# Decay sums by a scan, wider score products, and w_out buffers in turn, in a one-layer hybrid decoder step

## The chip, the cores and the metric

The kernel runs on one core of a Trainium2 chip. The metric is the device time of one execution in microseconds (us), the median of several runs. TensorE multiplies matrices (PE in the profile, with its weight loads as PEld), VectorE (DVE) and ScalarE (ACT) work elementwise, GpSimd (POOL) copies and fills, and SyncE (SP) issues most DMA transfers. PE writes to PSUM; the other engines move results from there to SBUF.

## The reference

One layer of a decoder on 512 prompt tokens and 8 × 4 sample tokens, in fp32: a half-step SwiGLU FFN, a mixing stage, and a second FFN, each closed by a layer norm. The mixing stage projects each token to `r`, `k`, `v`, low-rank gates and a short convolution's inputs, and runs a recurrence over time in each of 8 heads of 64 features:

```python
w_log = -softplus(-(w0 + tanh(wd) @ w_lora_up)) - 0.5
decay = exp(-exp(w_log))                  # = exp(-exp(-0.5) * sigmoid(w0 + tanh(wd) @ w_lora_up))
a = sigmoid(a0 + ad @ a_lora_up)
kk = k * k_k;  kk = kk / max(norm(kk), 1e-12)
S = S * decay + (S @ -kk) (kk * a)^T + v k^T       # per token and head
o = S @ r
```

The heads' outputs are normalised, gated, joined with the convolution's and multiplied by `w_out`.

## The kernel before

Features lie on the 128 partitions and the 544 token columns on the free axis; time columns are handled in halves of 256 and 288. To keep fp32 accuracy, each large operand is split in a high and a low part (`hl` for weights: ACT copies the high part, DVE subtracts for the low part, lines 146 and 147), and three products are summed. Weights come raw by DMA into `raw` tiles, and their split goes to the next `hl` tile of a ring: three base tiles, and extra ones while other memory is free. The ring's counter is `wstate["hl"]`.

PSUM has two rings: `mm` with three buffers (function `big`) and `sm` with five (function `sm`). A buffer is taken again only when its contents have been moved out.

The middle stage (about 395 to 728 us of the span) does the recurrence in chunks of 64 tokens, eight chunks and one set of sample columns. Its heads are taken in four pairs; the two heads of a pair (two "parities") lie in the lower and upper 64 partitions. For each pair the class `Pair` has these steps:

- `gates`: the decay's logits and `a`, from the low-rank rows `T12` and the weights `lo`. The decay's logits have time on the partitions; `w0`, copied to all partitions by a DMA, is added by DVE. ACT takes sigmoids (`sw`, `sws` for samples, `a`).
- `square`: the key's norm. ACT squares `k`, PE sums over a head, DVE takes a maximum; the tile is `kq`.
- `decays`: sums of the sigmoids within a chunk, as products of `sw` with triangular matrices `tri` and `tris`, then exponentials of both signs (`Pi`, `Pn`).
- `prep`: nine DVE instructions that scale key and `r` by them: `at`, `O`, `AR` for the samples, and `bkb`.
- `scores`: for each chunk and parity, `bkb` (weights) times `at` and times `O`. DVE masks the result from PSUM into `SC`, then scales `bkb` in place; PE then transposes `v` and the scaled `bkb`, and ACT moves those out (`UV`, `BK`).

Projections `project` run between these steps: `own_a(p+1)` (gates, k, square, r of the next pair) before `scores(p)`, `own_b(p+1)` (decays, prep, v) behind it. Pieces of projections or convolution are taken as fill between the pinned score steps. The program gives PE's order for pinned parts; for the rest the framework's scheduler sets each engine's order. Within an engine instructions run in the order set.

Behind the last scores come a triangular inverse on DVE with the sample tokens and the convolution beside it (`elim`, `sample`), the chain of eight chunks (`chain`), and `w_out` with the norm of the heads (`wout`, `gnorm`). Eight `w_out` weight blocks (`wc`, `wr`) are loaded and split there.

Of the kernel before, what the change touches and what calls it, by code (L numbers as in the profile page):

```python
# [61 lines left out]
def body(ctx: ExitStack, tc: tile.TileContext, xT, gu1, wd1, win, wo_c, wo_r, gu2, wd2, lora, w0, vec, cst,  # L62
# [764 lines left out]
    class Pair:  # L827
# [4 lines left out]
        def gates(self):  # L832
            p, fc = self.p, self.fc
            self.sw = sw = p2.tile([P, 4, P], F32, name="sw")
            self.sws = sws = p2.tile([64, P], F32, name="sws")
# [1 line left out]
            q, q2, qa = sm(), sm(), []
            for (t0, t1, h) in SEG:
                qa.append(sm())
                PE.matmul(qa[h][:, :t1 - t0], lo[64:128, 0, fc], T12[64:128, t0:t1], start=True, stop=True)  # L840
# [3 lines left out]
            DVE.tensor_tensor(sw, q.rearrange("p (t f) -> p t f", t=4), w0b[:, None, fc].to_broadcast([P, 4, P]), op=OP.add)  # L844
            DVE.tensor_tensor(sws, q2[0:64, 0:P], w0b[0:64, fc], op=OP.add)
            for t0, t1, h in SEG:
                ACT.activation(a[:, t0:t1], qa[h][:, :t1 - t0], AF.Sigmoid, bias=col(V_A0, p))
            ACT.activation(sw, sw, AF.Sigmoid)
            self.sg = ACT.activation(sws, sws, AF.Sigmoid)
# [9 lines left out]
        def decays(self):  # L859
            p, kq = self.p, self.kq  # L860
            Pi = p2.tile([P, 600], F32, name="Pi")
            self.Pn = Pn = p2.tile([P, 576], F32, name="Pn")
# [9 lines left out]
            ln_exp(self.sg, lambda: ACT.activation(pi[:, :, 1:65], s64(q), AF.Exp, scale=-CDEC))
            ACT.activation(ps_[:, :, 1:5], s4(q2[:, 0:64]), AF.Exp, scale=-CDEC)
            ACT.activation(Pn[:, 0:512], q, AF.Exp, scale=CDEC)
            ACT.activation(Pn[:, 512:576], q2[:, 0:64], AF.Exp, scale=CDEC)
# [1 line left out]
            ACT.activation(kq, kq, AF.Exp, scale=-0.5)
# [4 lines left out]
        def prep(self):
            p, nk, a, Pn = self.p, self.kq, self.a, self.Pn
            pi, ps_ = self.pi, self.ps
            self.at = at = p2.tile([P, 512], F32, name="at")
# [8 lines left out]
            DVE.tensor_tensor(O[:, p, 0:8, :], s64(rf[:, :512]), pi[:, :, 1:65], op=OP.mult)
# [5 lines left out]
            DVE.scalar_tensor_tensor(Pn, rf, col(V_RK, p), kf, op0=OP.mult, op1=OP.mult)  # L900
# [466 lines left out]
def _constants():  # L1367
# [77 lines left out]
```

## Time and profile before

| | us |
|---|---|
| median of three runs | 1105.9 (1105.31 to 1106.1) |
| the profiled execution | 1107.86 |
| its span | 1106.1 |
| PE busy | 1078.5 |
| DVE busy | 833.0 |
| ACT busy | 570.7 |
| gates of pair 0 to its scores | 406.5 to 432.3 |
| scores of pairs 1, 2, 3 begin | 468.0, 504.4, 528.6 |
| inverse, samples, convolution end | 601.2 |
| chunk chain ends | 645.5 |

In rows of the timeline a line has start, length, engine, source line, operation, output and inputs, shapes, count, and in square brackets the idle time before it with what ended it. A PE matmul in fp32 appears as two records. The names `T` and `cpb` in the gates' rows are the tiles `T12` and `lo`.

### The profile page before, as it was taken

How to read it: one execution, taken by the hardware profiler on the slowest of the kernel's cores; microseconds unless marked ns; L12 is line 12 of the kernel's file. 1: busy time of each engine (PE TensorE's matmuls, PEld its weight loads, DVE VectorE, ACT ScalarE, POOL GpSimd, SP SyncE). 2: the span in 40 equal slices, each digit the busy share in tenths (PEclk: the TensorE clock that was granted, in tenths of full speed). 3: DMA queues.
4: the chain of work that ended last, by engine and by line, in shares of the span. 5: the costliest groups of instructions: out<-in, count | busy, mean ns of one | idle time of the engine just before them, and what ended most of it. 6: DMA issues, size and time to landing. Idle time of an engine off the chain costs nothing.

```text
span 1106.1 us, 22515 instructions
## 1 busy us (share of the span) xinstructions
PE 1078.5 (98%) x9176; PEld 1035.7 (94%) x9176; DVE 833.0 (75%) x1520; ACT 570.7 (52%) x1042; POOL 201.9 (18%) x320
## 2 busy tenths in 40 slices
PE   9999999999999999999999999999999999999996
PEld 8999999999999998999879789899999999999995
DVE  7788888888875757668576477768889788886655
ACT  6645555564553575644222564467555556554524
POOL 0121221312100022212141610001312223031000
PEclk9999999999999999999999999999999999999998
DMA  8567594957742232122525333133957759495402
GB/s 289 123 134 193 120 221 102 213 143 163 187 126 91 95 107 68 39 68 70 135 70 152 126 111 115 49 105 77 212 140 160 177 125 214 126 196 132 115 1 81
DMA packets 81977, 142.98 MB, mean 129 GB/s; under 512 B 20432, under 2 KB 44368, under 8 KB 81616
## 3 DMA queue, kind: packets, MB, share of 16 engines
q1 hardware_dynamic: 54672, 105.35, 29.9%
q0 software_dynamic: 27200, 36.18, 21.0%
q8 instruction: 72, 1.18, 0.4%
q14 instruction: 33, 0.27, 0.1%
HBM read 123.65 MB, written 8.95 MB: 120 GB/s over the span
## 4 chain that ended last, share of the span: by engine, by line
PE 78%; DMA 7%; DVE 6%; ACT 4%; issue 4%; SPq 0%; POOL 0%; ACTq 0%; DVEq 0%; POOLq 0%
PE mm L75 50%; PE sm L75 29%; DMA z<-cpb 2%; DMA raw<-in_gu 2%; DVE hl L147 2%; ACT hl L146 2%; DMA z<-sv 1%; DMA raw<-in_wo_r 1%; DVE hhl L151 1%; DMA raw<-in_wd 1%; DMA z<-in_xT 1%; DVE z L609 0%; SPq L697 0%; DMA BK<-in_w 0%; ACT z L252 0%
## 5 line engine op out<-in xcount | busy, mean ns | idle before, releaser
L75 PE MATMUL mm<-xhl,hl 128*128 128x288 f32 (+2 forms) x2640 | 367.9, 294 | 0.9 <-ACT xhl L150 0.5
L75 PEld LDWEIGHTS mm<-xhl,hl 128*128 128x128 f32 x2640 | 344.7, 190 | 13.2 <-issue 5.4
L147 DVE TENSOR_TENSOR hl<-raw,hl 128x1024 fp32r<-128x1024 f32 (+3 forms) x224 | 261.0, 1170 | 67.7 <-ACT hl L146 66.7
L146 ACT ACTIVATE hl<-raw 128x1024 fp32r<-128x1024 f32 (+3 forms) x224 | 224.6, 1012 | 92.0 <-DVE raw L486 31.3
L75 PE MATMUL sm<-xhl,hl 128*128 128x272 f32 (+1 forms) x1392 | 193.8, 289 | 1.0 <-ACT xhl L150 0.7
L75 PEld LDWEIGHTS sm<-xhl,hl 128*128 128x128 f32 x1392 | 182.3, 189 | 2.2 <-ACT xhl L150 1.4
L75 PE MATMUL mm<-tv,hl 128*128 128x272 f32 x864 | 121.5, 289 | 4.1 <-ACT cpb L580 2.1
L75 PE MATMUL mm<-hhl,hl 128*128 128x272 f32 (+2 forms) x792 | 119.2, 294 | 0.1
L75 PEld LDWEIGHTS mm<-tv,hl 128*128 128x128 f32 x864 | 113.6, 189 | 5.2 <-ACT cpb L580 3.0
L75 PEld LDWEIGHTS mm<-hhl,hl 128*128 128x128 f32 x792 | 105.9, 188 | 5.1 <-ACT sv L625 1.5
L75 PE MATMUL sm<-hhl,hl 128*128 128x272 f32 (+2 forms) x792 | 109.6, 288 | 0.0
L75 PEld LDWEIGHTS sm<-hhl,hl 128*128 128x128 f32 x792 | 103.0, 188 | 0.5
L492 POOL DMA_DIRECT2D raw<-in_gu x36 | 43.5, 1209 | 258.4 <-DVE cpb L582 83.4
L498 POOL DMA_DIRECT2D raw<-in_wd x32 | 39.3, 1467 | 274.5 <-DVE hlb L151 240.2
L75 PE MATMUL mm<-tv,hlb 128*128 128x272 f32 x432 | 61.1, 291 | 0.7 <-ACT cpb L589 0.7
L75 PEld LDWEIGHTS mm<-tv,hlb 128*128 128x128 f32 x432 | 56.4, 188 | 2.3 <-ACT cpb L589 2.2
L150 ACT ACTIVATE hhl<-sv 128x272 fp32r<-128x272 f32 (+1 forms) x52 | 26.0, 513 | 30.3 <-DVE sv L349 12.1
L151 DVE TENSOR_TENSOR hlb<-raw,hlb 128x512 fp32r<-128x512 f32 x52 | 35.8, 688 | 5.6 <-ACT hlb L150 5.5
L150 ACT ACTIVATE hhl<-hk 128x272 fp32r<-128x272 f32 (+1 forms) x48 | 24.2, 505 | 27.5 <-DVE hk L556 12.9
L217 ACT ACTIVATE lnq<-z 128x512 f32<-128x512 f32 (+1 forms) x24 | 15.1, 654 | 42.9 <-DVE z L216 42.9
L486 DVE TENSOR_TENSOR raw<-raw 128x512 f32<-128x512 f32 x52 | 35.8, 689 | 1.0
L75 PE MATMUL mm<-hhl,hlb 128*128 128x272 f32 (+2 forms) x264 | 36.4, 288 | 0.0
(300 smaller groups left out, 1373.0 us busy)
## 6 DMA issues: line engine op xcount, KB each, us to landing
raw<-in_gu SPq DMA_DIRECT2D x84, 512.0 KB, 4.8
raw<-in_gu POOLq DMA_DIRECT2D x36, 512.0 KB, 6.4
raw<-in_wd SPq DMA_DIRECT2D x32, 512.0 KB, 4.6
raw<-in_win SPq DMA_DIRECT2D x26, 512.0 KB, 3.6
raw<-in_wd POOLq DMA_DIRECT2D x32, 256.0 KB, 6.4
raw<-in_wd SPq DMA_DIRECT2D x16, 384.0 KB, 3.2
z<-cpb POOLq DMA_DIRECT2D x16, 272.0 KB, 9.1
z<-sv POOLq DMA_DIRECT2D x16, 272.0 KB, 6.6
```

The costliest lines, as they stand in the source:

```text
L75: ins = f(*args, **kw)
L146: ACT.activation(hl[:, 0, a:b], raw[:, a:b], AF.Copy)
L147: DVE.tensor_tensor(hl[:, 1, a:b], raw[:, a:b], hl[:, 0, a:b].bitcast(F32), op=OP.subtract)
L150: ACT.activation(hi, x, AF.Copy)
L151: DVE.tensor_tensor(lo, x, hi.bitcast(F32), op=OP.subtract)
L217: sq = ACT.activation(qq, zz, AF.Square)
L486: DVE.tensor_tensor(y[:, :, 0], y[:, :, 1], a[:, :, 1], op=OP.add)
L492: POOL.dma_start(x.rearrange("p (s c) -> p s c", s=2), bass.AP(tensor=a11.tensor, offset=a11.offset, ap=[[2 * D, P], [P * 2 * D, 2], [1, 5 ...
L498: POOL.dma_start(four(x)[:, i], bass.AP(tensor=a11.tensor, offset=a11.offset, ap=[[DFF, P], [P * DFF, 2], [1, 256]]), accum_op=OP.add)
```

## The change

1. **Gates and decays.** The decay's logits are made in feature rows, as `a` already was, by two products of 256 and 320 columns. `w0` comes as a bias per feature of the sigmoid, so its DMA and the two additions on DVE go. One `tensor_tensor_scan` on DVE over 128x576 then sums the sigmoids along time: it multiplies the running sum by `cm`, which is 0 at each chunk's start and 1 elsewhere, and adds the next element. The triangular products and the constants for them go; `Exp` reads SBUF, and `Pn` is one instruction in place of two.
2. **Scores.** `at` and `O` lie in one tile `AO` (row 0 and rows 1 to 4), and each chunk and parity has one product with 128 columns, made of two strided pieces of 64, in place of two with 64.
3. **Value transposes** take one `mm` and one `sm` buffer in place of two `sm`.
4. **`own_a`** puts the first half of the `r` projection ahead of `square`.
5. **`wstate["hl"]`** is set to 0 ahead of the w_out loads and again ahead of the second FFN, so these blocks begin with the base tiles.

```diff
     def gates(self):
-            self.sw = sw = p2.tile([P, 4, P], F32, name="sw")
-            self.sws = sws = p2.tile([64, P], F32, name="sws")
+            self.sg = sg = p2.tile([P, 576], F32, name="sg")
...
-                for t in (2 * h, 2 * h + 1):
-                    PE.matmul(q[:, t * P:(t + 1) * P], T12[0:64, t * P:(t + 1) * P], lo[0:64, 0, fc], start=True, stop=True)
-            PE.matmul(q2[0:64, 0:P], T12[0:64, 512:576], lo[0:64, 0, fc], start=True, stop=True)
-            DVE.tensor_tensor(sw, q.rearrange("p (t f) -> p t f", t=4), w0b[:, None, fc].to_broadcast([P, 4, P]), op=OP.add)
-            DVE.tensor_tensor(sws, q2[0:64, 0:P], w0b[0:64, fc], op=OP.add)
...
+            for t0, t1, _ in SEG:
+                qw, qa = sm(), sm()
+                PE.matmul(qw[:, :t1 - t0], lo[0:64, 0, fc], T12[0:64, t0:t1], start=True, stop=True)
+                PE.matmul(qa[:, :t1 - t0], lo[64:128, 0, fc], T12[64:128, t0:t1], start=True, stop=True)
+                ACT.activation(sg[:, t0:t1], qw[:, :t1 - t0], AF.Sigmoid, bias=col(V_W0, p))
+                self.last = ACT.activation(a[:, t0:t1], qa[:, :t1 - t0], AF.Sigmoid, bias=col(V_A0, p))
+            DVE.tensor_tensor_scan(sg, cm, sg, 0.0, op0=OP.mult, op1=OP.add)
     def decays(self):
-            q = sm()
-            for t in range(4):
-                PE.matmul(q[:, t * P:(t + 1) * P], self.sw[:, t, :], tri, start=True, stop=True)
-            q2 = sm()
-            PE.matmul(q2[:, 0:64], self.sws, tris, start=True, stop=True)
...
+            ln_exp(self.last, lambda: ACT.activation(pi[:, :, 1:65], s64(self.sg[:, 0:512]), AF.Exp, scale=-CDEC))
+            ACT.activation(ps_[:, :, 1:5], s4(self.sg[:, 512:576]), AF.Exp, scale=-CDEC)
+            ACT.activation(Pn, self.sg, AF.Exp, scale=CDEC)
     def scores(self):
-                    for i, x in enumerate((at, O[:, p])):
-                        for par, q in enumerate(qs):
-                            PE.matmul(q[:, c * P + 64 * i:c * P + 64 * i + 64], bkb[R(par), a0c + c, :, :],
-                                      x[R(par), a0c + c, :], start=True, stop=True)
+                    for par, q in enumerate(qs):
+                        PE.matmul(q[:, c * P:c * P + P], bkb[R(par), a0c + c, :, :], AO[R(par), 0:p + 2:p + 1, a0c + c, :],
+                                  start=True, stop=True)
...
             for a0c, n in ((0, 5), (5, 4)):
-                qs = (sm(), sm())
+                qs = (big(), sm())
     def own_a(p):
+        yield from project(i + 1, p, 0, rf)
         yield from act(pairs[p].square)
-        yield from seq(*(project(i + 1, p, h, rf) for h in range(2)))
+        yield from project(i + 1, p, 1, rf)
...
+    wstate["hl"] = 0
     wc = [wload(wo_c[i]) for i in range(4)]
     wr = [wload(wo_r[i]) for i in range(4)]
...
     drain()
+    wstate["hl"] = 0
     wstate["ex_hl"] = []
```

The edits also move instructions. The first place is PE from the gates of pair 0 to those of pair 1. Before:

```order
L75 MATMUL sm<-T_4312,cpb 128x256
L75 MATMUL sm<-cpb,T_4312 128x128 x2
L75 MATMUL sm<-T_4312,cpb 128x320
L75 MATMUL sm<-cpb,T_4312 128x128 x2
L75 MATMUL sm<-cpb,T_4312 64x128
L75 MATMUL sm<-kq,cs 128x256
L75 MATMUL sm<-kq,cs 128x320
L75 MATMUL mm<-xhl,hl 128x288 x7
L75 MATMUL sm<-cs,sw 128x128 x4
L75 MATMUL sm<-cs,sws 128x64
L75 MATMUL mm<-xhl,hl 128x288 x17
L75 MATMUL sm<-T_4312,cpb 128x256
```

and with the change:

```order
L76 MATMUL sm<-T_4312,cpb 128x256 x2
L76 MATMUL sm<-T_4312,cpb 128x320 x2
L76 MATMUL sm<-kq,cs 128x256
L76 MATMUL sm<-kq,cs 128x320
L76 MATMUL mm<-xhl,hl 128x288 x24
L76 MATMUL sm<-T_4312,cpb 128x256 x2
```

The triangular products between the 7 and the 17 projection products are gone, and the time-row products (`cpb,T`) are feature-row products of the form that `a` had.

The second place is DVE at the scores of pair 1 (`SC` rows), with steps of pair 2 around them; `kq` and `r` are pair 2's. Before:

```order
L857 TENSOR_SCALAR kq<-sm 128x320
L786 SCALAR_TENSOR_TENSOR r<-pb,vc,dt 128x256
L887 SCALAR_TENSOR_TENSOR kq<-k,vc,kq 128x576
L786 SCALAR_TENSOR_TENSOR r<-pb,vc,dt 128x256
L790 SCALAR_TENSOR_TENSOR r<-pb,vc,dt 128x32
L147 TENSOR_TENSOR hl<-raw,hl 128x1024
L917 TENSOR_TENSOR SC<-sm,cs 128x512 x2
L147 TENSOR_TENSOR hl<-raw,hl 128x1024
L917 TENSOR_TENSOR SC<-sm,cs 128x512 x2
L917 TENSOR_TENSOR SC<-sm,cs 128x128 x2
L921 TENSOR_TENSOR bkb<-bkb,Pe 128x1024
```

and the same place with the change:

```order
L854 TENSOR_SCALAR kq<-sm 128x320
L877 SCALAR_TENSOR_TENSOR kq<-k,vc,kq 128x576
L879 SCALAR_TENSOR_TENSOR AR_4711<-kq,Pi 128x64
L787 SCALAR_TENSOR_TENSOR r<-pb,vc,dt 128x256
L791 SCALAR_TENSOR_TENSOR r<-pb,vc,dt 128x32
L884 TENSOR_TENSOR AO<-r,Pi 128x512
L885 TENSOR_TENSOR AR_4711<-r,Pi 128x64
L148 TENSOR_TENSOR hl<-raw,hl 128x1024
L905 TENSOR_TENSOR SC<-sm,cs 128x512 x4
L905 TENSOR_TENSOR SC<-sm,cs 128x128 x2
L909 TENSOR_TENSOR bkb<-bkb,Pe 128x1024
```

`AO<-r,Pi` (the former `O<-r,Pi`) and two small `AR` steps of pair 2 stand ahead of the score evictions; before, they stood behind `bkb<-bkb,Pe`. The weight split that stood between the evictions is gone from there, and one stands ahead of them as before. At the scores of pair 0 a split stands between the evictions in both kernels, at those of pair 2 none does with the change.

More of the change, by code (lines that the diff above doesn't have):

```diff
@@ L50 @@
 V_MU, V_A0, V_KK, V_KA, V_RK, V_GNG, V_GNB, V_CW = 48, 62, 66, 70, 74, 78, 82, 86
-NV = 98
-C_ONES, C_ID, C_MASK, C_MASKS, C_TRI, C_TRIS, C_BO, C_CEN, C_BM, C_OFF = 0, 128, 192, 320, 448, 576, 640, 768, 896, 904
-NCST = 968
+V_W0 = 98
+NV = 102
+C_ONES, C_ID, C_MASK, C_MASKS, C_BO, C_CEN, C_BM = 0, 128, 192, 320, 448, 576, 704
+NCST = 712
 def R(par):
@@ L61, in body @@
 @with_exitstack
-def body(ctx: ExitStack, tc: tile.TileContext, xT, gu1, wd1, win, wo_c, wo_r, gu2, wd2, lora, w0, vec, cst,
+def body(ctx: ExitStack, tc: tile.TileContext, xT, gu1, wd1, win, wo_c, wo_r, gu2, wd2, lora, vec, cst,
          sst, cstate, s0, y_o, wkvp_o, wkvs_o, shift_o, conv_o):
@@ L810, in body @@
     bo, cen, ident, msk, msks = (csl(c, n) for c, n in ((C_BO, P), (C_CEN, P), (C_ID, 64), (C_MASK, 128), (C_MASKS, 128)))
-    tri, tris, bmask, _ = csl(C_TRI, 128), csl(C_TRIS, 64, slice(0, 64)), csl(C_BM, 8), csl(C_OFF, 64)
-    O = tl([P, 4, NC_, 64], F32, name="O")
+    bmask = csl(C_BM, 8)
+    AO = tl([P, 5, NC_, 64], F32, name="AO")
+    at, O = AO[:, 0, 0:8], AO[:, 1:5]
     AR8 = tl([P, 4, 2, 64], F32, name="AR8")
@@ L820, in body @@
     UV = rc([P, 4, 2, NC_, 64], F32, name="UV")
-    w0b = BK[:, 3].rearrange("p a c t -> p (a c t)")[:, 0:512]
-    dma(w0b, bass.AP(tensor=w0.tensor, offset=w0.offset, ap=[[0, P], [1, 512]]))
+    cm = p2.tile([P, 576], F32, name="cm")
+    POOL.memset(cm, 1.0)
+    POOL.memset(cm[:, 0:512:64], 0.0)
+    POOL.memset(cm[:, 512:576:4], 0.0)
     Ad = dr.tile([2, 32, 65, 64], F32, name="Ad")
@@ L833, in gates @@
             p, fc = self.p, self.fc
-            self.sw = sw = p2.tile([P, 4, P], F32, name="sw")
-            self.sws = sws = p2.tile([64, P], F32, name="sws")
+            self.sg = sg = p2.tile([P, 576], F32, name="sg")
             self.a = a = p2.tile([P, 576], F32, name="a")
[L837 to L840, printed above, removed]
-                for t in (2 * h, 2 * h + 1):
-                    PE.matmul(q[:, t * P:(t + 1) * P], T12[0:64, t * P:(t + 1) * P], lo[0:64, 0, fc], start=True, stop=True)
-            PE.matmul(q2[0:64, 0:P], T12[0:64, 512:576], lo[0:64, 0, fc], start=True, stop=True)
[L844 to L849, printed above, removed]
+            for t0, t1, _ in SEG:
[5 more added lines that the diff above has]
+            DVE.tensor_tensor_scan(sg, cm, sg, 0.0, op0=OP.mult, op1=OP.add)
         def square(self):
@@ L871, in decays @@
             POOL.memset(ps_[:, :, 0], 1.0)
[L872 to L875, printed above, removed]
+            ln_exp(self.last, lambda: ACT.activation(pi[:, :, 1:65], s64(self.sg[:, 0:512]), AF.Exp, scale=-CDEC))
+            ACT.activation(ps_[:, :, 1:5], s4(self.sg[:, 512:576]), AF.Exp, scale=-CDEC)
+            ACT.activation(Pn, self.sg, AF.Exp, scale=CDEC)
             ACT.activation(kq, kq, AF.Ln)
@@ L884, in prep @@
             pi, ps_ = self.pi, self.ps
-            self.at = at = p2.tile([P, 512], F32, name="at")
             self.bkb = bkb = p2.tile([P, NC_, 2, 64], F32, name="bkb")
             DVE.scalar_tensor_tensor(nk, kf, col(V_KK, p), nk, op0=OP.mult, op1=OP.mult)
-            DVE.scalar_tensor_tensor(s64(at), s64(nk[:, :512]), -1.0, pi[:, :, 0:64], op0=OP.mult, op1=OP.mult)
+            DVE.scalar_tensor_tensor(at, s64(nk[:, :512]), -1.0, pi[:, :, 0:64], op0=OP.mult, op1=OP.mult)
             DVE.scalar_tensor_tensor(s4(AR8[:, p, 0, :]), s4(nk[:, 512:]), -1.0, ps_[:, :, 0:4], op0=OP.mult, op1=OP.mult)
             for par in range(2):
-                POOL.tensor_copy(UV[R(par), p, par, 0:8, :], s64(at)[R(par)])
+                POOL.tensor_copy(UV[R(par), p, par, 0:8, :], at[R(par)])
             DVE.tensor_tensor(nk, nk, a, op=OP.mult)
@@ L903, in scores @@
             p, bkb, vf = self.p, self.bkb, vfs[self.p]
-            at = s64(self.at)
             for a0c, n in ((0, 4), (4, 4), (8, 1)):
@@ L1376, in _constants @@
     blk = np.kron(np.eye(2), np.ones((64, 64)))
-    c[:, C_TRI:C_TRI + 128] = blk * np.tile(incl, (2, 2))
-    c[0:64, C_TRIS:C_TRIS + 64] = incl & same
     c[:, C_CEN:C_CEN + 128] = np.eye(P) - blk / 64
```

4 lines of the change are left out of this document (1 added, 3 removed).

## The prediction

> **What bounds the kernel now.** I read the page's busy shares first, then the chain of waits as shares by engine.
>
> ```profile
> PE 1078.5 (98%) x9176; PEld 1035.7 (94%) x9176; DVE 833.0 (75%) x1520; ACT 570.7 (52%) x1042; POOL 201.9 (18%) x320
> PE 78%; DMA 7%; DVE 6%; ACT 4%; issue 4%; SPq 0%; POOL 0%; ACTq 0%; DVEq 0%; POOLq 0%
> ```
>
> TensorE is nearly always busy, but an average over 1106 us says little about the stages that the change touches. So next the busy times by stretch: the run-up to the scores of head pair 0, one row from each pair's scores to the next pair's, the chunk chain, and the first half of w_out. The columns are length, then busy time and count of PE, weight loads, DVE, ACT and POOL, then clock, DMA share, GB/s.
>
> ```profile
> 406.50:432.30 25.80, 23.34 (x175) 21.22 (x174) 16.75 (x31) 17.08 (x35) 7.67 (x21) 1.00 0.17 52
> 432.30:468.00 35.70, 35.46 (x326) 33.09 (x325) 22.79 (x39) 19.72 (x44) 7.97 (x26) 1.00 0.18 53
> 468.00:504.40 36.40, 36.16 (x332) 33.79 (x331) 23.61 (x40) 19.54 (x42) 6.56 (x25) 1.00 0.22 67
> 504.40:528.60 24.20, 23.99 (x241) 22.58 (x241) 21.83 (x38) 10.85 (x24) 6.67 (x14) 1.00 0.26 61
> 601.20:645.50 44.30, 41.27 (x936) 35.96 (x935) 20.57 (x60) 21.96 (x67) 23.81 (x58) 1.00 0.28 88
> 645.50:682.50 37.00, 35.84 (x249) 32.85 (x247) 31.05 (x65) 22.83 (x43) 0.00 (x0) 1.00 0.37 118
> ```
>
> From 432 to 528 PE leaves under 0.3 us idle per row: what is taken from PE there comes off the end, unless a new wait eats it. In the first row PE idles 2.46 us, and the chain of waits names why:
>
> ```profile
> 406.62 3.28 DMA BK<-in_w
> 428.93 0.78 ACT kq L853
> ```
>
> The w0 rows arrive 3.3 us after PE needs them, everything of pair 0 on DVE and ACT is late by that, and PE ends up waiting at 429.75 for the square of pair 1's key. PE's own timeline around pair 0:
>
> ```profile
> 406.52 0.48 PE L75 MATMUL sm<-T,cpb 64*128 64x256 f32 x1
> 407.33 0.43 PE L75 MATMUL sm<-T,cpb 64*128 64x320 f32 x1
> 408.05 1.24 PE L75 MATMUL sm<-kq,cs 128*128 128x256 f32 x4
> 411.40 1.16 PE L75 MATMUL sm<-cs,sw 128*128 128x128 f32 x8 [1.18 <-ACT sw L848]
> 412.85 2.51 PE L75 MATMUL mm<-xhl,hl 128*128 128x288 f32 x17
> 429.75 1.24 PE L75 MATMUL sm<-kq,cs 128*128 128x256 f32 x4 [1.27 <-ACT kq L853]
> 432.29 0.44 PE L75 MATMUL sm<-at,bkb 64*128 64x64 f32 x4
> 435.69 0.39 PE L75 MATMUL sm<-O,bkb 64*128 64x64 f32 x4
> 435.91 0.44 PE L75 MATMUL sm<-AR,bkb 64*128 64x128 f32 x4
> 436.29 0.98 PE L75 MATMUL mm<-xhl,hl 128*128 128x256 f32 x6
> 440.26 0.53 PE L75 MATMUL sm<-cs,bkb 64*128 64x64 f32 x10
> 442.77 1.05 PE L75 MATMUL sm<-cs,sw 128*128 128x128 f32 x8
> 444.12 8.08 PE L75 MATMUL mm<-xhl,hl 128*128 128x256 f32 x61
> ```
>
> **The triangular products (decays).** From the first `sw` row to the next projection row: 444.12 − 442.77 = 1.35 us of PE, nothing beside it. The three later pairs each have this block, and each gives it back: −4.0 us. The clock is 1.00 in these stretches, so no share of it is throttle.
>
> **The gates.** Now 408.05 − 406.52 = 1.53 us. The two 256-column records start 0.32 us apart, the 320-column ones 0.27; with the time-row products gone, gates end where the last 320-column record ends its 0.27, at 407.60: 1.08 us. That is −0.45 for each of pairs 2 and 3 (pairs 0 and 1 belong to the run-up): −0.9.
>
> **The run-up to scores(0).** PE sheds 0.45 twice and the block 411.40 to 412.85 with its wait, so it would reach the second key square near 423.3. But that square waits for ACT, so I follow DVE and ACT. The w0 transfer and two adds go; the scan comes. The rows of the adds and of the key's last normalising step, from the timelines of DVE and ACT:
>
> ```profile
> 410.00 0.69 DVE L844 TENSOR_TENSOR sw<-sm,BK 128x512 f32<-128x512 f32 x1 [1.69 <-DMA BK<-in_w]
> 410.60 0.27 DVE L845 TENSOR_TENSOR sws<-sm,BK 64x128 f32<-64x128 f32 x1
> 414.78 0.69 ACT L877 ACTIVATE kq<-kq 128x576 f32<-128x576 f32 x1
> ```
>
> No scan is in this trace. The nearest row is a three-operand DVE instruction over the same 128x576, the first of these groups (busy time, then mean ns of one); the other rows are used further down:
>
> ```profile
> L900 DVE SCALAR_TENSOR_TENSOR Pn<-r,vc,k 128x576 f32<-128x576 f32 x4 | 3.2, 810 | 0.0
> L917 DVE TENSOR_TENSOR SC<-sm,cs 128x512 f32<-128x512 f32 x16 | 10.3, 684 | 2.7 <-PE sm L75 2.7
> L917 DVE TENSOR_TENSOR SC<-sm,cs 128x128 f32<-128x128 f32 x8 | 1.9, 282 | 0.0
> L921 DVE TENSOR_TENSOR bkb<-bkb,Pe 128x1024 f32<-128x1024 f32 x4 | 4.9, 1216 | 0.0
> L147 DVE TENSOR_TENSOR hl<-raw,hl 128x1024 fp32r<-128x1024 f32 x14 | 17.1, 1221 | 1.8 <-ACT hl L146 1.8
> L894 DVE TENSOR_TENSOR O<-r,Pi 128x512 f32<-128x512 f32 x4 | 2.7, 684 | 1.9 <-ACT Pi L872 1.9
> ```
>
> I bound the scan between 0.8 us and twice that, 1.6, and take 1.2 (it does one multiply and one add per element, but each needs the one before). [...] Sigmoids end near 409.0, the scan near 410.3, exponentials and key normalisation near 413.3 in place of 415.4, and pair 0's nine DVE instructions, the second scan and two weight splits follow without a gap. The second square comes at about 427 in place of 429.75, and PE then has 17 fill matmuls before the scores, as now. Scores(0) start near 429.8 in place of 432.29: **−2.5** (−1 if pair 1's exponentials fall behind a weight split of 1.2 us, −4 if the scan costs 0.8 and nothing else queues).
>
> **The scores.** Sixteen groups from 432.29 to 435.91 are 0.226 us each, one group being one 64-column operand, two parities, two records per matmul. What sets 0.226 us is not the streaming: the `sw` block runs 8 records of 128 columns in 0.99 us, 0.124 each, while a score group runs 2 records per row half in 0.226, 0.113 each with half the columns. So a 128-column group should cost about 0.224, eight of them 1.79 us in place of 3.62: −1.83 per pair, −7.3 in all on PE alone. The other bound is the `AR` group, 128 columns in the same row halves: 436.29 − 435.91 = 0.38, eight of them 3.04, −0.6 per pair. [...]
>
> But **PE is not alone there**. Behind each pair's scores DVE has, in order, four evictions of 128x512 (pitch 0.64 us), two of 128x128 (0.2), and the scaling of `bkb` (1.2); PE's transposes of `bkb` need the last one, and the sixth `sm` buffer needs the first eviction since the ring has five. Before:
>
> ```profile
> 434.45 1.28 DVE L917 TENSOR_TENSOR SC<-sm,cs 128x512 f32<-128x512 f32 x2
> 438.37 1.21 DVE L921 TENSOR_TENSOR bkb<-bkb,Pe 128x1024 f32<-128x1024 f32 x1
> 468.29 0.49 DVE L786 SCALAR_TENSOR_TENSOR r<-pb,vc,dt 128x256 f32<-128x256 f32 x1 [1.25 <-ACT dt L785]
> ```
>
> DVE is done with pair 0 at 439.58, 0.7 us before PE's transposes at 440.26. After the change PE would be there 5.2 us after the scores' start (scores 1.8, AR 0.4, 18 fill matmuls 2.4, values 0.6) in place of 7.97. DVE won't: the order of the changed kernel puts `O` of the next pair (0.6), which waits for the `r` eviction, ahead of the first score eviction, and in pairs 0 and 1 a weight split (1.2) too. First eviction after the scores' start, then `bkb` scaled: pair 0, 2.45 (behind the key's 0.8, `r` and `O`) + 1.3 + 0.2 + 1.2 + 1.7 + 1.2 = 8.0; pair 1, `r` at 0.7, `O`, split, so 3.15, + 3.0 + 1.2 = 7.3; pair 2, 1.7 + 1.3 + 0.7 (a conv row) + 1.7 + 1.1 = 6.5; pair 3, with nothing ahead, 1.1 + 3.0 + 1.1 = 5.25. The same path before: 7.97, 8.1, 7.7 and 7.2. Fill matmuls that stood in it and stand elsewhere now (5, 5, 2, 1 at 0.118) come off the gain. Net: +0.7, −0.2, −1.0, −1.8: **−2.4** instead of −7.3. So most of the scores' saving becomes a wait of PE for DVE.
>
> **w_out and the rest.** Three of the eight splits are done before or in the chunk chain and not behind it. One of them stands inside the chain, 1.1 us on ACT and 1.2 on DVE, in a stretch where PE idles 3.0 us. Behind it these waits of PE may go:
>
> ```profile
> 646.89 0.74 PE L75 MATMUL mm<-xhl,hl 128*128 128x256 f32 x4 [0.25 <-ACT hl L146]
> 647.84 0.50 PE L75 MATMUL mm<-xhl,hl 128*128 128x256 f32 x2 [0.21 <-ACT hl L146]
> 667.63 0.62 PE L75 MATMUL mm<-xhl,hl 128*128 128x256 f32 x3 [0.47 <-ACT xhl L150]
> ```
>
> They sum to 0.9 us, and PE idles 1.2 in that row. I take 0 (−1.5 to +1.5). The inverse's 64 us only move earlier.
>
> **Sum** against the profiled 1107.86 us: −4.0 − 0.9 − 2.5 − 2.4 ± 0 = −9.8, so 1098.1 profiled. The median of the runs, 1105.9, lies 2 us lower, and I forecast **1096 us** for it.
>
> **Rivals.**
> 1. *PE alone decides*: DVE's evictions keep up, since DVE is 64% busy there (22.79 of 35.70). Then −7.3 for the scores, −1.2 for the transposes that no longer wait, with the other terms −15.9: 1090. For it: PE's idle is now near zero. Against: the order on DVE. Chance 0.24.
> 2. *More waits than I count*: the run-up gives 1, the scores nothing, the chain costs 1.5: −4.0 − 0.9 − 1 + 1.5 = −4.4, 1101.5. For it: DVE's rows above are in series with PE in three pairs. Chance 0.16.
> 3. *128 columns cost what the AR row says*: 1.25 us more per pair on PE. In pairs 0 to 2 DVE is later anyway, in pair 3 it costs about 1: 1097, inside my forecast's own range (1093 to 1099).
> 4. *Slower: the scan is the bound.* A running sum needs each element's predecessor. Each of the first two is on the path at its full price. The other two stand where the sums `sw` stood, and DVE idles next:
>
> ```profile
> 458.27 0.48 DVE L786 SCALAR_TENSOR_TENSOR k<-pb,vc,dt 128x256 f32<-128x256 f32 x1 [2.83 <-POOL car L788]
> ```
>
> At 5 us per scan the gain is gone: 2 × 3.8 for the first two, and 2 × (3.8 − 2.8) for the others, 9.6; at 6 us it is 13.6, which makes 1110. Against: 5 us would be six times the nearest row. Chance 0.05.
> 5. *Nothing measurable*: rival 2's waits with a scan of 3 us, −4.4 + 2 × 1.8 = −0.8: 1105. Chance 0.05.
>
> **The numbers.** My forecast has 0.50. Range 1088.5 to 1101.5: it takes in rival 1 and reaches to rival 2. About 2 us (0.2%) is what runs of this kernel can tell from no change. Faster 0.90, same 0.05, slower 0.05.
>
> **What would show it.** No `sw` products; scan rows of 0.8 to 1.6 us; key square of pair 1 near 427; eight score groups 0.224 us apart (0.33 to 0.38 by rival 3) with a gap before the AR row and another before `cs,bkb`, both released by DVE, about 3 us in pair 0, 2.3 in pair 1, under 0.5 in pair 3. By rival 1 those gaps are missing and the rows of 36 us become 31.7; by mine they become 33 to 35. I am wrong if the gaps are absent, or the chain's 44.3 us change by over 1.5.

## The result, and the profile after

The changed kernel takes 1098.55 us (median of four runs, 1097.42 to 1099.9) against 1105.71 us: a ratio of 0.9936, with a 95% interval of 0.9919 to 0.9953. It is faster by 7.2 us. The forecast was 1096, with a range of 1088.5 to 1101.5. A second series of runs of the same kernel gave 1098.78 us and a ratio of 0.9938 (0.9918 to 0.9959). Three single executions far above the rest (1292.32 and 5830.42 us of the kernel before, 1463.42 us of the one with 128-column scores alone) are left out of all medians and ratios below.

The busy shares and the shares of the chain of waits, from the page of the changed kernel:

```profile
PE 1067.4 (97%) x8984; PEld 1024.7 (93%) x8984; DVE 833.5 (76%) x1516; ACT 570.4 (52%) x1038; POOL 206.6 (19%) x323
PE 85%; DVE 6%; DMA 3%; ACT 3%; issue 2%; SPq 0%; POOL 0%; ACTq 0%; DVEq 0%; POOLq 0%
```

PE lost 11.1 us of work, but the span only 9.1, so about 2 us turned into waiting. The busy times by stretch, from the gates of pair 0 to its scores, then from one pair's scores to the next, the last from pair 3's scores to the inverse (columns as in the prediction):

```profile
407.66:433.59 25.93, 22.48 (x152) 20.19 (x151) 18.50 (x30) 18.94 (x39) 8.93 (x24) 0.93 0.11 41
433.59:466.55 32.96, 31.71 (x277) 29.58 (x276) 22.64 (x39) 18.61 (x40) 7.07 (x26) 1.00 0.19 57
466.55:500.17 33.62, 32.35 (x283) 30.27 (x282) 23.49 (x39) 19.50 (x41) 7.60 (x26) 1.00 0.23 72
500.17:522.63 22.46, 21.10 (x199) 19.65 (x198) 19.85 (x36) 9.02 (x20) 7.11 (x13) 1.00 0.27 65
522.63:533.93 11.30, 9.33 (x93) 7.67 (x92) 5.57 (x9) 3.92 (x9) 1.44 (x4) 0.85 0.44 137
```

PE's idle, under 0.3 us per row before, is now 1.25, 1.27 and 1.36 us in the middle rows. In the first row it grew from 2.46 to 3.45 us, and the granted clock there is 0.93, in the last row 0.85; both were 1.00 before. Where the time of the two profiled executions went (us, starts of the rows that open each stage):

| stage | before | after | difference |
|---|---|---|---|
| start to gates of pair 0 (not touched) | 406.52 | 407.68 | +1.16 |
| gates to scores of pair 0 | 25.77 | 25.91 | +0.14 |
| scores 0 to scores 1 | 35.66 | 32.96 | −2.70 |
| scores 1 to scores 2 | 36.37 | 33.62 | −2.75 |
| scores 2 to scores 3 | 24.18 | 22.46 | −1.72 |
| scores 3 to the inverse | 9.77 | 11.30 | +1.53 |
| inverse, samples, convolution | 62.96 | 64.39 | +1.43 |
| chunk chain, to the first head norm | 46.95 | 47.53 | +0.58 |
| w_out first half, to the second layer norm | 42.19 | 40.25 | −1.94 |
| second layer norm to the end | 415.73 | 410.90 | −4.83 |

From the gates to the inverse that is 131.75 before and 126.25 after. PE's timeline of the changed kernel, for pair 0 and then the waits at the scores of pairs 1 and 3:

```profile
407.68 1.24 PE L76 MATMUL sm<-T,cpb 64*128 64x256 f32 x8
408.85 1.24 PE L76 MATMUL sm<-kq,cs 128*128 128x256 f32 x4
409.68 3.58 PE L76 MATMUL mm<-xhl,hl 128*128 128x288 f32 x24
...
428.67 2.29 PE L76 MATMUL sm<-kq,cs 128*128 128x256 f32 x4 [3.45 <-ACT kq L850]
430.29 3.37 PE L76 MATMUL mm<-xhl,hl 128*128 128x288 f32 x17
433.59 2.06 PE L76 MATMUL sm<-AO,bkb 64*128 64x128 f32 x32
435.47 0.38 PE L76 MATMUL sm<-AR,bkb 64*128 64x128 f32 x2
436.05 0.49 PE L76 MATMUL sm<-AR,bkb 64*128 64x128 f32 x2 [0.20 <-DVE SC L905]
...
440.74 0.52 PE L76 MATMUL sm<-cs,bkb 64*128 64x64 f32 x10 [1.03 <-DVE bkb L909]
441.76 1.24 PE L76 MATMUL sm<-Pn,cs 128*128 128x256 f32 x4
442.59 8.80 PE L76 MATMUL mm<-xhl,hl 128*128 128x256 f32 x66
...
470.06 0.48 PE L76 MATMUL sm<-AR,bkb 64*128 64x128 f32 x2 [1.24 <-DVE SC L905]
...
526.84 0.48 PE L76 MATMUL sm<-AR,bkb 64*128 64x128 f32 x2 [1.94 <-DVE SC L905]
527.25 1.54 PE L76 MATMUL mm<-xhl,hl 128*128 128x288 f32 x6
```

Projection work follows the `Pn` products directly; the triangular products are gone. Eight score groups take 435.47 − 433.59 = 1.88 us in place of 3.62. Behind them stand the new waits, all released by DVE. DVE's rows of the changed kernel at the scan, then at the scores of pair 0:

```profile
409.89 1.36 DVE L846 TENSOR_TENSOR_SCAN sg<-cm,sg 128x576 f32<-128x576 f32 x1 [0.43 <-ACT sg L844]
...
434.71 0.68 DVE L884 TENSOR_TENSOR AO<-r,Pi 128x512 f32<-128x512 f32 x1
435.31 1.28 DVE L905 TENSOR_TENSOR SC<-sm,cs 128x512 f32<-128x512 f32 x2
436.51 0.22 DVE L885 TENSOR_TENSOR AR<-r,Pi 128x64 f32<-128x64 f32 x1
436.65 1.22 DVE L148 TENSOR_TENSOR hl<-raw,hl 128x1024 fp32r<-128x1024 f32 x1
437.78 1.68 DVE L905 TENSOR_TENSOR SC<-sm,cs 128x512 f32<-128x512 f32 x4
439.38 1.22 DVE L909 TENSOR_TENSOR bkb<-bkb,Pe 128x1024 f32<-128x1024 f32 x1
```

The first eviction begins 1.72 us after the scores, behind `AO<-r,Pi`, and `bkb` is done at 440.60; PE resumes at 440.74.

One thing was in no step of the prediction. After the wait at 428.67 the four `kq` records take 1.62 us (to 430.29), where the first square's take 0.83 (408.85 to the next row at 409.68). The granted clock by single microseconds, same kernel:

```profile
427.00:428.00 1.00, 0.00 (x0) 0.00 (x0) 0.38 (x2) 0.52 (x2) 0.76 (x5) 1.00 0.77 307
428.00:429.00 1.00, 0.33 (x1) 0.33 (x2) 0.49 (x1) 0.62 (x1) 0.10 (x1) 0.80 0.41 115
429.00:430.00 1.00, 1.00 (x3) 0.82 (x3) 0.07 (x1) 0.00 (x0) 0.00 (x0) 0.50 0.72 295
430.00:431.00 1.00, 1.00 (x4) 0.61 (x4) 0.36 (x2) 0.00 (x0) 0.00 (x0) 0.50 0.34 139
431.00:432.00 1.00, 1.00 (x6) 1.00 (x6) 0.49 (x1) 0.42 (x1) 0.00 (x0) 0.50 0.00 0
432.00:433.00 1.00, 1.00 (x9) 1.00 (x9) 0.00 (x0) 0.96 (x2) 0.00 (x0) 0.99 0.00 0
```

TensorE runs at half clock for 3.41 us, from 428.61 to 432.02. That loses about 1.5 us: 0.8 at the four records, and 0.8 at the 17 products behind them, which take 3.30 us and would take 2.5 at the 3.58 us for 24 of the row at 409.68. Behind the wait at 526.84 the same happens again, from 527.60 to 531.01.

### The profile page after: what moved, and what is told of

Read it like the earlier page. It is cut to its first block, busy times and chain, and to the rows that moved or that the text cites. A ratio compares the mean times of both kernels' runs of the same rounds, so it can differ in the third digit from the quotient of the medians.

```text
span 1097.0 us, 22120 instructions
## 1 busy us (share of the span) xinstructions
PE 1067.4 (97%) x8984; PEld 1024.7 (93%) x8984; DVE 833.5 (76%) x1516; ACT 570.4 (52%) x1038; POOL 206.6 (19%) x323
## 4 chain that ended last, share of the span: by engine, by line
PE 85%; DVE 6%; DMA 3%; ACT 3%; issue 2%; SPq 0%; POOL 0%; ACTq 0%; DVEq 0%; POOLq 0%
PE mm L76 55%; PE sm L76 30%; DMA z<-sv 2%; DVE hl L148 1%; DVE SC L905 1%; ACT hl L147 1%; DMA raw<-in_wd 1%; DMA z<-in_xT 0%; SPq L698 0%; DMA raw<-in_gu 0%; DVE hhl L152 0%; POOL z L637 0%; ACT z L253 0%; DVE bkb L909 0%; DVE S L1058 0%
## 5 line engine op out<-in xcount | busy, mean ns | idle before, releaser
L76 PE MATMUL mm<-xhl,hl 128*128 128x256 f32 (+2 forms) x2640 | 368.6, 295 | 0.9 <-DVE hl L148 0.9
L76 PEld LDWEIGHTS mm<-xhl,hl 128*128 128x128 f32 x2640 | 345.7, 190 | 13.7 <-issue 6.7
```

What stands on the lines that cost most here:

```text
L76: ins = f(*args, **kw)
```

## The experiments

The stage lengths come from one profiled execution each; they are compared from the gates of pair 0 to the inverse. "Half clock" is the time in that stretch at a granted clock of 0.50. In these profiles it came in pieces of 3.41 us (in the changed kernel 428.61 to 432.02 and 527.60 to 531.01), which differed between executions of like kernels and cost about 1.4 us each (62.96 us for the inverse with one piece against 64.39 with two, further down), so stage lengths with different half clock need this taken off before they are compared. The ratio is against the kernel before, run beside each. Among the variants of the changed kernel only the one in bold has an interval that lies clear of the changed kernel's; what is said of the others rests on the stage lengths.

| kernel | median us | ratio (95%) | gates to scores 0 | gates to inverse | half clock |
|---|---|---|---|---|---|
| before | 1105.7 to 1106.7 | 1 | 25.77 | 131.75 | 0 |
| changed, first and second | 1098.55, 1098.78 | 0.9936, 0.9938 | 25.91, 25.90 | 126.25, 125.97 | 6.8, 6.8 |
| changed, without the second reset | 1097.14 | 0.9928 (0.9906 to 0.9949) | 27.12 | 128.45 | 13.7 |
| before with the resets alone | 1103.02 | 0.9975 (0.9957 to 0.9994) | 25.48 | 131.44 | 0 |
| changed, 64-column scores | 1096.51 | 0.9916 (0.9885 to 0.9947) | 25.83 | 124.99 | 3.4 |
| before, 128-column scores alone | 1101.66 | 0.9960 (0.9942 to 0.9978) | 25.49 | 128.91 | 3.4 |
| changed, squares behind the scores | 1096.68 | 0.9904 (0.9878 to 0.9930) | 19.63 | 122.02 | 6.8 |
| changed, evictions first | 1095.62 | 0.9915 (0.9894 to 0.9936) | 25.59 | 120.49 | 3.4 |
| changed, r before the square | 1096.11 | 0.9910 (0.9887 to 0.9934) | 22.85 | 123.98 | 6.8 |
| the same with idle products | 1097.19 | 0.9918 (0.9898 to 0.9939) | 22.85 | 124.77 | 6.8 |
| evictions first and r before | **1091.60** | **0.9860 (0.9839 to 0.9880)** | 24.71 | 119.35 | 3.4 |
| the same, 64-column scores | 1097.11 | 0.9927 (0.9898 to 0.9955) | 24.00 | 127.79 | 13.7 |
| evictions first, squares behind | 1096.37 | 0.9904 (0.9882 to 0.9926) | 19.97 | 120.38 | 3.4 |

### What the resets of the ring do

```diff
     drain()
-    wstate["hl"] = 0
     wstate["ex_hl"] = []
```

> The changed kernel without the counter's reset ahead of the second FFN; all else as changed. In the profiled executions the second FFN (from 726.7 before, 722.4 after, to the end) became 4.8 us shorter, which my sum did not hold. Theory A: the reset did it (the FFN's weight blocks begin with base tiles that are free earlier, so TensorE waits less for split weights): the time goes up by 3 to 5 us, to 1102 to 1103.5, and the waits of TensorE for the weight combinations of 1.4 and 1.9 us come back. Theory B: the waits there move from execution to execution with the transfers and the reset does nothing: 1098.5, within 1.5 us.

The time did not rise: 1097.14 us over twelve runs, a ratio of 0.9928 (0.9906 to 0.9949) against 0.9936 (0.9919 to 0.9953) with the reset. Theory A falls for the second reset: 3 to 5 us would show, though 1 or 2 would not. The stage from the second layer norm to the end took 410.2 to 416.3 us over fourteen profiled executions of kernels with and without the reset, 416.2 in this kernel (whose profiled execution was its slowest of the twelve, 1106.71 us) and 416.3 in one that has the reset, so the 4.83 us of the first comparison are no gain that can be put down to the edit. Part of the scatter is the clock: the three longest of the fourteen (415.73 to 416.34) each have two pieces of 3.41 us at half clock in that stage ahead of its last 10 us, the five with one took 410.90 to 414.66, and the six with none 410.24 to 413.84.

The kernel before with both resets and nothing else:

```diff
+    wstate["hl"] = 0
     wc = [wload(wo_c[i]) for i in range(4)]
...
     drain()
+    wstate["hl"] = 0
     wstate["ex_hl"] = []
```

> The kernel before with the two resets of the counter and nothing else. Theory A: the second FFN gains its 4 us and the w_out half its 2 us (the waits of 0.25, 0.21, 0.22 and 0.47 us at 646 to 668 are gone), less up to 1 us in the chunk chain: 1100 to 1101. Theory B: only the w_out part gains, less what the chain loses: 1104 to 1105.5.

0.9975 with an upper end of 0.9994 is a small gain, 3.0 us by the medians (1105.98 for the kernel before beside it). From the first head norm to the second layer norm it took 40.12 us against 42.19 before and 40.25 in the changed kernel, and the four waits of PE between 646 and 668 us are gone. All twelve profiles with the first reset have 40.04 to 40.29 there, the two without it 42.19 and 42.80. The first reset is worth 2 us there; neither theory had the total.

### Do the wide scores pay?

```diff
-                    for par, q in enumerate(qs):
-                        PE.matmul(q[:, c * P:c * P + P], bkb[R(par), a0c + c, :, :], AO[R(par), 0:p + 2:p + 1, a0c + c, :],
+                    for i, x in enumerate((at, O[:, p])):
+                        for par, q in enumerate(qs):
+                            PE.matmul(q[:, c * P + 64 * i:c * P + 64 * i + 64], bkb[R(par), a0c + c, :, :],
```

> The changed kernel with the score products taken back to two with 64 columns; all else as changed. If VectorE's evictions set the pace behind the scores, as I predicted, most of the 1.83 us that TensorE loses per pair comes out of its waits for VectorE (0.2 + 1.0, 1.2, 0.2 + 0.3, 1.9 us in pairs 0 to 3, the last with a halved clock behind it): 1099.5 to 1101, and the waits in front of the sample product are gone. If TensorE alone decides: 4 x 1.83 = 7.3 us more, 1105.9.

It cost nothing: 1096.51 us, and 124.99 us from the gates to the inverse. Two waits of PE are left in that stretch, and none of them is for an eviction:

```profile
427.41 1.24 PE L76 MATMUL sm<-kq,cs 128*128 128x256 f32 x4 [3.44 <-ACT kq L850]
509.61 12.41 PE L76 MATMUL mm<-xhl,hl 128*128 128x256 f32 x97 [0.42 <-DVE hl L148]
```

So within the changed kernel the wide products gain nothing that shows: some 7 us less work on PE (4 × 1.74) became 5.3 us more of waits for DVE, and the one in pair 3 brought a half clock with it. I had expected narrowing them to cost 1 to 2.5 us; it cost none.

In the kernel before, the wide products alone (same diff the other way round, with `at` and `O` in one tile):

> The kernel before with only the 128-column score products; VectorE keeps the order that it had (the evictions ahead of the next pair's product of r). Theory: eight groups in 1.8 to 1.9 us in place of 3.62, but VectorE hands over the scaled keys no earlier than 7.3, 7.4 and 6.9 us after the start of the scores in pairs 0 to 2 (before: 7.3, 7.4, 6.9), so TensorE gains about 0.65, 0.65 and 0.8 us there and 1.8 in pair 3: 3.9 us from the gates to the inverse, 131.75 to about 128, total 1101 to 1103. Rival (TensorE alone decides): 7.3 us, about 1098.

1101.66 us, and 128.91 us from the gates to the inverse, 2.84 less. DVE keeps its old order there, and PE waits for the first eviction in three pairs:

```profile
436.47 0.49 PE L75 MATMUL sm<-AR,bkb 64*128 64x128 f32 x2 [0.62 <-DVE SC L915]
...
471.70 0.48 PE L75 MATMUL sm<-AR,bkb 64*128 64x128 f32 x2 [0.82 <-DVE SC L915]
...
507.35 0.49 PE L75 MATMUL sm<-AR,bkb 64*128 64x128 f32 x2 [0.82 <-DVE SC L915]
```

Pair 3 has no such wait, as expected. TensorE alone does not decide; about 3 of 7 us come through even in the old order. One piece of half clock (from 509.65), which the kernel before does not have in this stretch, lies in the 128.91; without its 1.4 us the gain would be some 4.2, near the expected 3.9.

### Whose order holds PE up

```diff
+    keep_dve = tc.keep_in_program_order
...
-            DVE.tensor_tensor(O[:, p, 0:8, :], s64(rf[:, :512]), pi[:, :, 1:65], op=OP.mult)
+            keep_dve(DVE.tensor_tensor(O[:, p, 0:8, :], s64(rf[:, :512]), pi[:, :, 1:65], op=OP.mult))
```

The same is put around both `AR` steps, the `SC` evictions and the scaling of `bkb`; `prep` of the next pair comes later in the program, so it now runs behind them.

> The changed kernel with VectorE's order pinned at the scores: the evictions and the scaling of bkb come ahead of the next pair's product of r with the decays (0.6 us) and the sample products (0.2 us each). Theory (VectorE's order holds TensorE up behind the scores): the waits for the first eviction and for the scaled keys shrink from 0.2 + 1.0, 1.2 and 0.2 + 0.3 us in pairs 0 to 2 to under 0.5 us each, 1.5 to 2.5 us less in all; pair 3 stays. Rival: the evictions then wait for the weight split and for r as before, and the time moves by under 0.5 us.

5.5 us less from the gates to the inverse than in the second run of the changed kernel (120.49 against 125.97), and 1095.62 us. PE's waits from the gates on:

```profile
428.89 1.90 PE L76 MATMUL sm<-kq,cs 128*128 128x256 f32 x4 [3.12 <-ACT kq L852]
439.63 0.53 PE L76 MATMUL sm<-cs,bkb 64*128 64x64 f32 x10 [0.89 <-DVE bkb L911]
468.51 0.48 PE L76 MATMUL sm<-AR,bkb 64*128 64x128 f32 x2 [0.82 <-DVE SC L907]
501.77 0.49 PE L76 MATMUL sm<-AR,bkb 64*128 64x128 f32 x2 [0.82 <-DVE SC L907]
```

The waits for DVE, 5.7 us in the changed kernel, are 2.5. Two of the three left stand behind the weight split that still precedes the evictions, and none is under the 0.5 us that I had expected: in pairs 0 to 2 the waits for evictions and for `bkb` were 1.23, 1.24 and 0.48 us and are 0.89, 0.82 and 0.82 (the 0.86 us for a weight split in pair 2 is gone). I had expected pair 3 to stay: it gained most, 3.5 of the 5.5 us, since the weight split ahead of the evictions there is done at 519.91, before the scores begin at 520.32, and without that wait the clock stays at 1.00. In the changed kernel the rows of pair 3 on DVE are

```profile
524.96 1.23 DVE L148 TENSOR_TENSOR hl<-raw,hl 128x1024 fp32r<-128x1024 f32 x1 [4.61 <-ACT hl L147]
526.10 2.87 DVE L905 TENSOR_TENSOR SC<-sm,cs 128x512 f32<-128x512 f32 x6
```

and the scores began at 522.63: a split that waits 4.61 us for ACT's copy holds six evictions. So VectorE's order does hold PE up, but by these waits more through the weight splits than through the product of r that the edit moved.

### The wait for the square, and the clock

The first test moves the square of pair p+1 behind the scores of pair p:

```diff
     def own_a(p):
         yield from project(i + 1, p, 0, rf)
-        yield from act(pairs[p].square)
         yield from project(i + 1, p, 1, rf)
...
     def own_b(p):
+        yield from act(pairs[p].square)
         yield from act(pairs[p].decays)
```

> The changed kernel with the square of pair p+1's key moved from ahead of the scores of pair p to behind them; same work. Theory: the wait of 3.45 us for this square in pair 0 and the 3.3 us at clock 0.50 that follow it (1.65 us lost) are gone, so the scores of pair 0 begin 4 to 5 us earlier, 21 to 22 us after the gates in place of 25.9, and the total is 1093 to 1095. Rival: the scores of pair 0 then wait for something else of the same chain (the scaled keys on VectorE), or the late square delays the scores of pair 1: 1097 to 1099.

The scores of pair 0 begin 19.63 us after the gates, even earlier than expected, but part of it is lost directly behind: PE then waits 3.05 us for the first eviction, and the clock is at 0.50 from 430.65 to 437.48. The total is 1096.68 us, between what the theory and the rival had: the wait for the square and its clock were real, and a large part of them moved to DVE. The stretch from pair 0's scores to pair 1's is 4.4 us longer than in the changed kernel (37.37 against 32.95), of which 0.8 are the square's own products.

The second test puts all of pair 1's r projection ahead of its square, and a twin adds four products that nobody needs:

```diff
+        if p == 1:
+            yield from project(i + 1, p, 1, rf)
         yield from act(pairs[p].square)
-        yield from project(i + 1, p, 1, rf)
+        if p > 1:
+            yield from project(i + 1, p, 1, rf)
```

```diff
                 q = sm()
+                if self.p == 1 and t0 == 0:
+                    for _ in range(4):
+                        PE.matmul(q[:, :256], bo, T12[:, 0:256], start=True, stop=True)
                 PE.matmul(q[:, :t1 - t0], bo, kq[:, t0:t1], start=True, stop=True)
```

> The changed kernel with both halves of pair 1's r projection ahead of its key square, so TensorE has 11 more products before it waits. The wait shrinks from 3.45 to about 2.0 us, still long enough for the clock to fall to 0.50 behind it if a wait over about 1.7 us is what does that; gates to scores of pair 0 about 24 us in place of 25.9. If the wait is now too short, clock 1.00 and about 22.5 us.

> The kernel of rfirst with four more products of 256 columns, of no use, into the square's own buffer ahead of the square: 1.7 us of work in place of most of the wait. The rest is as in rfirst. Theory (the wait halves the granted clock for some 3.3 us): clock 1.00 behind it and scores of pair 0 earlier than in rfirst by 1.4 to 1.7 us although TensorE does more. Rival (the clock fell for another reason, or the square is not waited for): scores no earlier, or later by up to 1.7 us.

> The changed kernel itself, so that the next three stand beside it on one chip. From the gates of pair 0 to its scores 25.9 us as in its first profile, with the wait of 3.45 us for pair 1's key square and clock 0.50 behind it; total 1097 to 1099.

The kernel without idle products:

```profile
429.11 1.24 PE L76 MATMUL sm<-kq,cs 128*128 128x256 f32 x4 [1.99 <-ACT kq L850]
429.94 1.11 PE L76 MATMUL mm<-xhl,hl 128*128 128x256 f32 x6
```

and with them:

```profile
427.56 1.89 PE L76 MATMUL sm<-T,cs 128*128 128x256 f32 x8
429.71 1.24 PE L76 MATMUL sm<-kq,cs 128*128 128x256 f32 x4 [0.26 <-ACT kq L850]
```

The wait shrank to 1.99 us as expected, but the clock did not fall: four `kq` records took 0.83 us, and the scores of pair 0 begin 22.85 us after the gates. The 1.7 us above which a wait was to bring half clock was an estimate, and this run speaks against it. So there was no half clock for the idle products to prevent, both kernels have the square 20.98 us after the gates, and the twin shows only that filling a wait with 1.7 us of work that nobody needs costs nothing ahead of the square. What separates the changed kernel is clear all the same: it too has the square at 428.67 − 407.68 = 20.99 us, and needs 4.92 us from there to the scores, against 1.87. Eleven products fewer behind the square, at the 3.58 us for 24 of the row at 409.68, are 1.6 us of that; the other 1.4 are the clock. The second run of the changed kernel repeats its 25.90 us, with a wait of 3.43.

### A version that beats both

Both edits together, and the same with narrow scores:

> The changed kernel with VectorE's order pinned as in evict_first and pair 1's r projection ahead of its square as in rfirst. From the gates to the inverse evict_first took 120.5 us and rfirst 3.05 us less than the changed kernel ahead of the scores of pair 0. If the two gains are apart: 117.5 us there and 1092.5 to 1094 in all, under both kernels. If one takes from the other (VectorE ahead of the scores of pair 0 becomes later): 119 to 120.5 and 1095.

> evict_rfirst with the score products taken back to two of 64 columns. In the changed kernel that cost nothing (it was 1.3 us shorter from the gates to the inverse). Theory: with the evictions first TensorE waits less for VectorE, so the narrow products now cost 2 to 5 us from the gates to the inverse. Rival: VectorE still sets the pace and the two are within 1 us.

The first took 1091.60 us, a ratio of 0.9860 (0.9839 to 0.9880), 7 us under the changed kernel, and its interval lies wholly below the changed kernel's. The gains did not add up in the profile (119.35 us, not 117.5): with VectorE's new order the wait for the square is 2.48 us and the clock falls behind it again, so the scores of pair 0 come at 24.71 us.

```profile
428.10 2.03 PE L76 MATMUL sm<-kq,cs 128*128 128x256 f32 x4 [2.48 <-ACT kq L852]
437.63 0.52 PE L76 MATMUL sm<-cs,bkb 64*128 64x64 f32 x10 [0.49 <-DVE bkb L911]
466.56 0.49 PE L76 MATMUL sm<-AR,bkb 64*128 64x128 f32 x2 [0.82 <-DVE SC L907]
499.81 0.48 PE L76 MATMUL sm<-AR,bkb 64*128 64x128 f32 x2 [0.82 <-DVE SC L907]
```

With narrow scores it took 1097.11 us, 5.5 more by the medians; the intervals of the ratios do not overlap. Its profiled execution is the slowest of the seven (1106.12 us): the clock stayed at 0.50 from 430.83 to 444.48 us, through pair 0's scores, three pieces more than in the wide kernel. At 1.4 us each they make 4.2 of the 8.4 us between the two profiles, and the 4.2 left are inside the 2 to 5 expected. Whether the narrow products helped to keep the clock down was not tested. The wide scores pay once VectorE's evictions and r come first. The last combination:

> The changed kernel with the squares behind the scores as in square_late and VectorE's order pinned as in evict_first. square_late began the scores of pair 0 19.6 us after the gates but took 11.4 us from there to the transposed keys, with 5.3 us of waits for evictions. Theory: the pinned order takes most of those waits away, 115 to 118 us from the gates to the inverse and 1091 to 1094 in all. Rival: the scores of pair 0 begin before VectorE has done its weight splits and projections, and the waits stay: 120 to 122 us.

1096.37 us, and 120.38 us from the gates to the inverse: the rival was right. The scores begin 19.97 us after the gates, and PE then waits 2.77 us for the first eviction.

## Why the prediction was right, and where it was not

The direction, the size within its range, and the mechanism held: of the forecast's 9.8 us, 7.2 came. Point by point:

- **Triangular products.** Forecast −4.0. The rows are gone, and `Pn` is followed by projections 0.83 us later (441.76 to 442.59), where it took 2.42 us before (441.70 to 444.12). That held, and gave 1.59 us per pair where I had 1.35.
- **Gates.** Forecast 1.08 us, measured 408.85 − 407.68 = 1.17. That held.
- **The scan.** Bounds 0.8 and 1.6 us, taken 1.2, measured 1.36 for each of the four. That a scan costs up to twice the nearest row of that shape was an estimate, which no run had shown; against that row's 0.81 us it is a factor of 1.7. The slower rival is out.
- **Score products on PE.** Forecast 1.79 us for eight groups, measured 1.88; the `AR` row's 0.38 per group was the wrong price, and a wide group took nearly what a narrow one had taken (0.235 us against 0.226). Rival 3 is out.
- **DVE behind the scores.** From the scores' start to the transposes of `bkb` I had 8.0, 7.3, 6.5 and 5.25 us. The profile has 7.15, 7.20, 6.52 and 9.09. The first three are the mechanism as predicted, DVE's serial evictions with the next pair's `O` and weight splits in front; rival 1, PE alone, is out. The gaps of PE were smaller than the 3 and 2.3 us that I had named for pairs 0 and 1 (1.23 and 1.24), and larger than the 0.5 for pair 3 (1.94). The fourth path is the step that failed: "pair 3, with nothing ahead". A weight split stood ahead, late by itself.
- **The run-up.** I had the second key square near 427, 2.75 us earlier relative to the gates; it came at 20.99 us after them in place of 23.23, so 2.24 earlier. But the step "and PE then has 17 fill matmuls before the scores, as now" failed. Before, PE had 11 there, not 17:

```profile
430.58 1.78 PE L75 MATMUL mm<-xhl,hl 128*128 128x288 f32 x11
```

The square and 17 products take some 3.4 us at full clock (0.83 and 2.5), where I had 2.8 from 427 to 429.8; and they ran at half clock and took 4.92. So −2.5 became +0.14: 0.5 us by the later square, 0.6 by the products, 1.5 by the clock. The prediction had the wait itself and did not ask for the clock behind a wait of 3.4 us.
- **Two readings of the run-up.** The 423.3 at which PE "would reach the second key square" does not follow from its own terms: 429.75 − 1.27 − 0.9 − (1.45 + 1.18) makes 424.95, which is 18.4 us after the gates; PE was there 17.5 us after them. And DVE waited 1.69 us for the `w0` rows (the row at 410.00), not 3.3. No term of the sum hangs on either.
- **w_out.** Forecast 0 (−1.5 to +1.5). The part behind the chain gained 1.94, the chain lost 0.58: the wait terms were mis-sized, not the place. The chain's change is within the 1.5 us that I had set as a sign of being wrong.
- **The inverse** took 1.43 us more in the first profile and 62.95 us, as before, in the second. That is the clock in a stretch of tiny products, not the change: over all fourteen profiles this stage took 61.54 us in the one without half clock in it, 62.89 to 62.97 in the seven with one piece of 3.41 us, and 64.33 to 64.85 in the six with two. So a piece costs about 1.4 us.

Summed over the stages that the change touches (gates to the second layer norm), I had −9.8 us and the profiles have 278.42 − 283.85 = −5.43. The difference of 4.4 is the run-up (+2.6), the four pairs together (−5.6 in place of −7.3: pair 3's row fell short by 3.3, and the three rows before it gained 1.7 more than I had), the inverse (+1.4), the chain (+0.6) and w_out (−1.9). In the second profile of the changed kernel the same stages took 276.27 us, which is 7.58 less than before, so they can hold the whole of the 7.2 us between the medians; one profile is too little to share it out to 2 us. That the forecast came within 2.6 us of the median is in part luck: the run-up and pair 3 missed by 2.6 and 3.3 us, and gains that I had not counted stood against them. The stages ahead of the gates and behind the second layer norm moved by +1.16 and −4.83 us between the first two profiles; which of that would stay over many executions is open, and the run without the second reset shows no 3 to 5 us from that edit.

## What to carry to other kernels

When an engine that is nearly always busy is given less work, list the in-order queue of the engine that empties its buffers: here VectorE's row of evictions, with other work put in front by the scheduler, was the length of the stage. In the profiles of this stretch a new order there was worth 5.5 us (1.4 of them the clock's), the widened product some 3 in the old order and nothing in the changed one; in the total, only the new order together with r ahead of the square stands clear of the changed kernel. Price a wait with the clock behind it: here a gap of 3.45 us cost its own length and then 1.5 us more. Compare stages between fixed points of the program, and look at the clock in each, since stages that the change does not touch moved by several us from one execution to the next.

## What the runs showed of the hardware that I had not expected

The granted clock of TensorE fell to 0.50 behind all nine idle gaps of 2.48 to 3.45 us between the gates and the inverse; behind a gap of 1.99 us it stayed at 1.00, but behind one of 1.94 us in pair 3 it fell. The same wait of 1.24 us at pair 1's scores was followed by half clock in the kernel with idle products, where the 13 records of the second projection row behind it took 2.95 us, and not in the second profile of the changed kernel, where they took 1.80. So the length of the gap alone does not tell.

The traces' records of the clock show more. Leaving out the last 10 us, the stretches at 0.50 lasted 3.41, 6.83 or 13.65 us (428.61 to 432.02 and 548.08 to 554.90 in the changed kernel, 430.83 to 444.48 in the one with both edits and 64-column scores). Within one execution they began whole multiples of one step apart: in the changed kernel at 428.61, 527.60, 548.08, 612.93 and 708.50, which is 29, 6, 19 and 28 steps of 3.413 us (279.89 us in 82), and in the kernel before at 552.99, 713.42 and 1003.55, which is 47 and 85. So in these two executions the clock changed on a grid with that step. Where it lay against the program differed: the first stretch begins 20.93 us after the gates in the changed kernel and 21.38 in its second profile. The gap of 1.94 us lay whole in one step, and the next ran at half clock (columns as in the prediction):

```profile
524.19:527.60 3.41, 1.47 (x16) 1.16 (x13) 2.64 (x4) 1.12 (x2) 0.00 (x0) 1.00 0.18 61
527.60:531.01 3.41, 3.41 (x22) 2.85 (x21) 2.50 (x5) 0.87 (x2) 0.40 (x2) 0.50 0.84 229
```

The gap of 1.99 us, in the kernel with r before the square, is here in two rows of a step's length, 1.33 us of it in one and 0.66 in the other; the clock was 1.00 in both, and in the single microseconds behind them up to 437:

```profile
425.04:428.45 3.41, 2.08 (x16) 1.84 (x14) 2.78 (x5) 2.27 (x6) 3.16 (x8) 1.00 0.45 144
428.45:431.86 3.41, 2.75 (x24) 2.41 (x26) 2.50 (x7) 2.84 (x6) 0.61 (x4) 1.00 0.57 163
```

That the place of the grid is why the clock fell behind the one gap and not behind the other is a guess from one execution of each; it was not tested. Idle time is not all: in the changed kernel the clock also fell at 548.08, behind the samples' 128 records of 8 columns, and PE had been busy for all 3.41 us of the step before, from 544.67. What sets the clock was not settled.

Two 128-column products in opposite row halves took hardly more than two with 64 columns: 0.235 us per group (eight in 1.88 us) against 0.226.
